# Windowed attention: the value product of a block moves from three blocks behind its scores to four

## The chip, the cores and the metric

The kernel runs on one core of a Trainium2 chip. The metric is the device time of one execution in microseconds. Before the change its median over three runs is 2266.35 us (2261.28 to 2271.24). TensorE (PE) multiplies matrices, VectorE (DVE), ScalarE (ACT) and GpSimd (POOL) work on rows, SyncE (SP) issues most transfers, and sixteen DMA engines carry them out.

## The reference, cut to what matters

One inference step of a two-layer network over 128 context tokens and 1024 latent tokens. The first layer mixes a state-space scan with pooling; the second has eight heads of differential attention over all keys and sixteen heads of windowed attention with a sink. The change concerns the last of these. For latent tokens a query block of 128 sees the context keys and its own and the two neighbouring key blocks:

```python
s_w = jnp.where(valid, s_w, NEG_INF)
s_c = jnp.einsum('bkgqd,bkld->bkgql', qb, k_ctx).astype(jnp.float32) * scale
logits = jnp.concatenate([s_c, s_w, jnp.broadcast_to(sk, s_c.shape[:-1] + (1,))], axis=-1)
p = jax.nn.softmax(logits, axis=-1).astype(v.dtype)
return (jnp.einsum('bkgql,bkld->bkgqd', p[..., :n_ctx], v_ctx)
        + jnp.einsum('bkgqw,bkwd->bkgqd', p[..., n_ctx:n_ctx + 3 * WIN_BLK], vw))
```

Context tokens attend to context tokens alone, with the same sink. Nothing of what is computed changes.

## The kernel before

The program is one long stream. The first layer takes about the first 950 us, its output projection and the start of the second layer follow; the eight dense (differential) heads run from about 1027 to 1697 us, the windowed heads, here called the sliding stage, from about 1698 to 2066 us, and the last output projection fills the rest.

**Numbers in two halves.** fp32 values are kept as a pair of fp16 tiles, high and low, and a product is three fp16 matmuls (`mm3`, lines 326 to 331, or the like). So a block of probabilities has a high and a low half.

**The sliding stage** is eight calls of `win_block` (line 1343), one for each pair of heads (`m` = 0, 1). A call walks nine query blocks, b0 (context) to b8. For each block TensorE makes the scores of both heads (lines 1367 and 1370), VectorE adds the mask and takes the extreme (1378; 1375 for b0), ScalarE takes exponentials into the fp32 tile `p` (1380), then copies `p` to fp16, the high half (1389), and GpSimd subtracts to get the low half (1390); both lie in `phl`. SyncE then issues a DMA transpose of `phl` into a tile `PT` (`transpose`, line 1233), of 4, 12 or 16 blocks of 128 x 128. Last, TensorE multiplies `PT` with the values (`win_pv`, lines 1407 to 1409) and ScalarE writes the result, scaled by the softmax's divisor, to `og` (1411). A finished pair is gated and written to DRAM (`go_dr`, line 1260).

**The lag.** The value product is not made at once. `win_block` puts it on the list `pend` (line 1392) and, in each block after the scores, calls `self.pop(2)`, which makes the oldest products until two are left. So in block b the product of block b - 3 is made. The list goes on over the change of pair.

**The filler.** Between these, TensorE is given slices of other projections (`F.take`), from a list of jobs: the next pair's Q first (`qk_block`, line 1158), then the gates (`z_block`). TensorE's order is as written; on the other engines a scheduler sets the order when the program is built, from its own estimate and from marks of priority. Each engine then runs its list strictly in order and waits by semaphores.

**The next pair's Q.** `qk_block` ends with four transfers on SyncE's queue (line 1198) that bring the finished Q, as `qhl`, into the layout that the scores need: two for `m` = 0 and then two for `m` = 1. They are called pieces 1 to 4. A score of head `m` reads all 128 partitions of `Q[:, m]`, so `m` = 0 needs pieces 1 and 2, `m` = 1 pieces 3 and 4.

**Buffers.** Tiles with one tag share a ring: before the change three of `p` (also used by the dense heads, line 1277, and by `cached_values`), three of `phl` and three of `PT`. A writer waits until the last reader of the ring's tile has finished.

Of the kernel before, what the change touches and what calls it, by code (L numbers as in the profile page):

```python
# [10 lines left out]
F32 = mybir.dt.float32  # L11
F16 = mybir.dt.float16
# [7 lines left out]
P = 128  # L20
TC = 128
TL = 1024
T = TC + TL
# [6 lines left out]
TK = T + TC  # L30
# [190 lines left out]
class Builder:  # L221
# [925 lines left out]
    def cached_values(self):  # L1147

        nc, A = self.nc, self.A
        self.cv = self.wt([P, 2, 10, P], F16, tag="cv", bufs=1)  # L1150
        cvf = self.cv.rearrange("p a b c -> p a (b c)")
        for c in (slice(0, TK // 2), slice(TK // 2, TK)):
            t = self.wt([P, T], F32, tag="p", bufs=3)[:, :TK // 2]
            nc.sync.dma_start(t, A["cv"][:, c])
            nc.scalar.activation(cvf[:, 0, c], t, AF.Copy)
            nc.vector.tensor_tensor(cvf[:, 1, c], t, cvf[:, 0, c], ALU.subtract)
# [71 lines left out]

    def transpose(self, phl, nb):

        pt = self.wt([P, 18, P], F16, tag="PT", bufs=3)
        with self.tc.high_priority():
            self.last_t = self.nc.sync.dma_start_transpose(pt[:, :nb], phl).ins
        if self.loads:
            with self.tc.issue_after(self.last_t):
                self.loads.popleft()()
        return pt
# [24 lines left out]
    def diff_head(self, h, F):  # L1262

        nc = self.nc
        F.until(("k", h))
        F.until(("q", h))
        k, q = self.R.pop(("k", h)), self.R.pop(("q", h))
        og = self.wt([P, NCH, P], F32, tag="og", bufs=3)
        oss = self.wt([P, 16], F32, tag="oss", bufs=2)
        left = F.left - (HEAD_KEEP if h < 7 else HEAD_LAST)  # L1270
        for b in range(NCH):
            nk = 1 if b == 0 else 9
            w = nk * P
            o = TC if b else 0
            qs = slice(b * P, (b + 1) * P)
            sm = self.wt([P, 16], F32, tag="sms", bufs=6)
            e = self.wt([P, T], F32, tag="p", bufs=3)[:, :w]


            for ms in ((0,), (1,)) if b else ((0, 1),):  # L1280
                st = self.pt("S", [P, 1536])
                out = self.pend.popleft()(st) if ms[0] == 0 and len(self.pend) > 2 else None
                sv = st[:, :len(ms) * w].rearrange("p (a b) -> p a b", b=w)
                for i, m in enumerate(ms):
                    for c0 in range(0, w, 512):
                        c1 = min(c0 + 512, w)
                        for x in range(2):
                            nc.tensor.matmul(sv[:, i, c0:c1], q[:, m, x, qs], k[:, m, o + c0:o + c1], start=x == 0, stop=x == 1)  # L1288
                with self.tc.high_priority():
                    nc.vector.tensor_reduce(out=sm[:, ms[0]:ms[-1] + 1], in_=sv, axis=AX.X, op=ALU.max, negate=True)  # L1290
                    for i, m in enumerate(ms):
                        nc.scalar.activation(sv[:, i] if m else e, sv[:, i], AF.Exp, bias=sm[:, m:m + 1],
                                             accum_out=sm[:, 4 + m:5 + m])
                if out is not None:
                    out()
                F.take(left / 16 if b else 2 * HEAD_FIRST)
            p = [e, sv[:, len(ms) - 1]]

            phl = self.wt([P, 2 * T], F16, tag="phl", bufs=3)
            with self.tc.high_priority():  # L1300
                nc.vector.reciprocal(sm[:, 6:8], sm[:, 4:6])
                nc.vector.scalar_tensor_tensor(sm[:, 2:3], sm[:, 4:5], self.nlam, sm[:, 7:8], ALU.mult, ALU.mult)
                nc.vector.scalar_tensor_tensor(p[0], p[1], sm[:, 2:3], p[0], ALU.mult, ALU.add)  # L1303
                nc.scalar.activation(phl[:, :w], p[0], AF.Copy)  # L1304
            nc.gpsimd.tensor_tensor(phl[:, w:2 * w], p[0], phl[:, :w], ALU.subtract)  # L1305
            pt = self.transpose(phl[:, :2 * w], 2 * nk)
            self.pend.append(lambda st=None, b=b, nk=nk, pt=pt, sm=sm: self.diff_pv(st, h, b, nk, pt, sm, og, oss))
# [35 lines left out]
    def win_block(self, qb, F):  # L1343

        nc = self.nc
        F.until(("wk", qb // 4))
        F.until(("q", 8 + qb))
        k, q = self.R["wk", qb // 4], self.R.pop(("q", 8 + qb))
        og = self.wt([P, NCH, P], F32, tag="og", bufs=3)
        kv = (qb // 2) % 2  # L1350
        fill = F.left / (2 * NCH - 2 + 2 * WIN_FIRST)
        for b in range(NCH):
            qs = slice(b * P, (b + 1) * P)
            if b == 0:
                lo, hi, nk, mk = 0, TC, 1, None
            else:
                lo, hi = max(b - 1, 1) * P, min(b + 2, NCH) * P
                nk = (hi - lo) // P + 1
                mk = self.mask[:, 1:4] if b == 1 else self.mask[:, 4:7] if b == 8 else self.mask[:, 0:4]
            w = nk * P  # L1360
            wl = hi - lo
            sm = self.wt([P, 16], F32, tag="sms", bufs=6)
            p = self.wt([P, T], F32, tag="p", bufs=3)[:, :2 * w]
            for m in range(2):
                s = self.pt("S1")
                for x in range(2):
                    nc.tensor.matmul(s[:, :wl], q[:, m, x, qs], k[:, kv, lo:hi], start=x == 0, stop=x == 1)  # L1367
                if b:
                    for x in range(2):
                        nc.tensor.matmul(s[:, wl:w], q[:, m, x, qs], k[:, kv, T:TK], start=x == 0, stop=x == 1)  # L1370
                nsk = self.nsink[:, 2 * qb + m:2 * qb + m + 1]
                nb = sm[:, m:m + 1]
                with self.tc.high_priority():
                    if mk is None:
                        nc.vector.tensor_reduce(out=nb, in_=s[:, :w], axis=AX.X, op=ALU.min)
                        nc.vector.tensor_tensor(nb, nb, nsk, ALU.min)
                    else:
                        nc.vector.tensor_tensor_reduce(out=s[:, :w], in0=s[:, :w], in1=mk.rearrange("p a b -> p (a b)"),  # L1378
                                                       scale=1.0, scalar=nsk, op0=ALU.add, op1=ALU.min, accum_out=nb)
                    nc.scalar.activation(p[:, m * w:(m + 1) * w], s[:, :w], AF.Exp, bias=nb, scale=-1.0,  # L1380
                                         accum_out=sm[:, 4 + m:5 + m])
                    nc.scalar.activation(sm[:, 6 + m:7 + m], self.row("sink", 2 * qb + m, 1), AF.Exp, bias=nb)  # L1382
            F.take(fill * WIN_FIRST if b == 0 else fill + WIN_SHIFT)
            self.pop(2)
            F.take(fill * WIN_FIRST if b == 0 else fill - WIN_SHIFT)
            nc.vector.tensor_reduce(out=sm[:, 2:4], in_=sm[:, 4:8].rearrange("p (a b) -> p b a", a=2), axis=AX.X, op=ALU.add)
            nc.vector.reciprocal(sm[:, 8:10], sm[:, 2:4])
            phl = self.wt([P, 2 * T], F16, tag="phl", bufs=3)
            nc.scalar.activation(phl[:, :2 * w], p, AF.Copy)  # L1389
            nc.gpsimd.tensor_tensor(phl[:, 2 * w:4 * w], p, phl[:, :2 * w], ALU.subtract)  # L1390
            pt = self.transpose(phl[:, :4 * w], 4 * nk)
            self.pend.append(lambda b=b, nk=nk, pt=pt, lo=lo, sm=sm: self.win_pv(qb, b, nk, lo, pt, sm, og))
# [262 lines left out]
```

## Time and profile before

| | us |
|---|---|
| median of three runs | 2266.35 (2261.28 to 2271.24) |
| profiled execution | 2267.45 |
| its span, first to last instruction | 2265.7 |
| mean granted TensorE clock | 0.957 |
| TensorE matmuls busy | 2022.8 (89%) |
| VectorE, ScalarE, GpSimd busy | 1467.3, 1224.6, 1062.4 |

A row of a group reads: line, engine, operation, what it writes and reads, count, busy time, mean of one in ns, idle time of the engine before it and what ended that. A row of time reads: start, duration, engine, line, operation; in brackets the idle time of the engine just before it and what released it. A row of a stretch reads: from:to, its length, busy time and count of PE, PEld, DVE, ACT and POOL, granted clock, share of the sixteen DMA engines, GB/s. A busy TensorE is not TensorE at its peak. SPq is SyncE's queue: the duration there is that of issuing, not of the transfer.

### The profile page before, as it was taken

To read this page: it belongs to the slowest core of one execution; us is meant where nothing else is said; L and a number is where in the kernel's file an instruction comes from. 1 tells how busy PE (TensorE), PEld (TensorE's weight loads), DVE (VectorE), ACT (ScalarE), POOL (GpSimd) and SP (SyncE) were. 2 spreads that over 40 slices of the span, in tenths; PEclk is the share of its full clock that TensorE was granted. 3 is DMA by queue.
4 is the path that set the end of the run, shared out by engine and by line. 5 is a ranking of instruction groups with operands and counts; after the bars stand their busy time and mean duration, and the time that the engine had idled before them with its cause. 6 is when DMAs were issued, how large, how long until landed. Compare 5 with 4: busy or idle time off the path is not lost. (4 is left out here: it accounts for less than half of the span.)

```text
span 2265.7 us, 49724 instructions
## 1 busy us (share of the span) xinstructions
PE 2022.8 (89%) x20258; PEld 1438.0 (63%) x20258; DVE 1467.3 (65%) x2722; ACT 1224.6 (54%) x2891; POOL 1062.4 (47%) x997
## 2 busy tenths in 40 slices
PE   5996788787989999998998998999889998998997
PEld 2654475564557655665676786776667777686566
DVE  5868989789586444675777767767755544552334
ACT  5565667566564322344665665565557867782321
POOL 1369677876675100144445445445346756651001
PEclk9998999998999999998999999999989999999999
DMA  7221523224657513034455555555457878899312
GB/s 277 73 81 48 138 72 99 77 89 127 198 205 209 184 66 109 26 124 109 103 121 115 113 120 114 111 116 120 103 117 133 170 148 157 167 175 216 139 47 84
DMA packets 435125, 283.10 MB, mean 125 GB/s; under 512 B 374448, under 2 KB 385232, under 8 KB 434896
## 3 DMA queue, kind: packets, MB, share of 16 engines
q1 hardware_dynamic: 433920, 279.34, 49.7%
q8 instruction: 158, 2.59, 0.5%
q10 hardware_dynamic: 976, 0.58, 0.1%
q14 instruction: 71, 0.58, 0.1%
HBM read 133.38 MB, written 29.05 MB: 72 GB/s over the span
## 5 line engine op out<-in xcount | busy, mean ns | idle before, releaser
L329 PE MATMUL psmm<-h,whl 128*128 128x384 f16 (+1 forms) x1104 | 367.8, 334 | 21.0 <-DVE q L1175 14.7
L330 PE MATMUL psmm<-h,whl 128*128 128x384 f16 (+1 forms) x1104 | 367.7, 334 | 2.3 <-DVE h L506 1.7
L331 PE MATMUL psmm<-h,whl 128*128 128x384 f16 (+1 forms) x1104 | 367.2, 333 | 0.0
L329 PE MATMUL psmm<-whl,h 128*128 128x128 f16 x1920 | 336.1, 221 | 10.4 <-DVE V L1211 10.4
L330 PE MATMUL psmm<-whl,h 128*128 128x128 f16 x1920 | 336.0, 221 | 0.0
L331 PE MATMUL psmm<-whl,h 128*128 128x128 f16 x1920 | 335.9, 221 | 0.0
L330 PEld LDWEIGHTS <-whl 128*128 128x128 f16 x2256 | 224.5, 100 | 165.2 <-issue 43.4
L331 PEld LDWEIGHTS <-whl 128*128 128x128 f16 x2256 | 224.4, 99 | 155.2 <-issue 15.8
L329 PEld LDWEIGHTS <-whl 128*128 128x128 f16 x2256 | 225.4, 100 | 145.7 <-issue 20.7
L1305 POOL TENSOR_TENSOR phl<-p,phl 128x1152 f16<-128x1152 f32 (+1 forms) x72 | 155.4, 2162 | 231.4 <-ACT phl L1304 231.4
L330 PEld LDWEIGHTS <-h 128*128 128x128 f16 x2520 | 247.5, 99 | 12.8 <-issue 11.1
L329 PEld LDWEIGHTS <-h 128*128 128x128 f16 x2520 | 247.5, 99 | 4.2 <-issue 2.6
L331 PEld LDWEIGHTS <-h 128*128 128x128 f16 x2520 | 247.5, 99 | 0.0
L323 DVE SCALAR_TENSOR_TENSOR whl<-w,whl 128x512 f16<-128x512 f32 x248 | 196.1, 809 | 64.5 <-ACT whl L322 63.5
L1290 DVE TENSOR_REDUCE sms<-psS 128x1 f32<-128x1152 f32 (+1 forms) x136 | 176.5, 1298 | 73.6 <-PE psS L1288 72.5
L1390 POOL TENSOR_TENSOR phl<-p,phl 128x1024 f16<-128x1024 f32 (+2 forms) x72 | 134.0, 1861 | 109.9 <-ACT phl L1389 77.4
L322 ACT ACTIVATE whl<-w 128x512 f16<-128x512 f32 x248 | 140.1, 609 | 79.2 <-PE psmm L331 42.6
L1288 PE MATMUL psS<-K,Q 128*128 128x512 f16 (+1 forms) x800 | 151.9, 326 | 32.1 <-DVE p L1303 17.1
L1180 POOL TENSOR_TENSOR sw<-sw,sin 128x384 f32<-128x384 f32 (+1 forms) x78 | 85.8, 1100 | 146.8 <-DVE sw L1179 128.0
L503 POOL TENSOR_TENSOR h<-mt,h 128x384 f16<-128x384 f32 (+2 forms) x32 | 29.1, 918 | 250.1 <-ACT h L502 250.1
L1288 PEld LDWEIGHTS <-Q 128*128 128x128 f16 x800 | 73.4, 99 | 100.5 <-DVE p L1303 18.1
L1304 ACT ACTIVATE phl<-p 128x1152 f16<-128x1152 f32 (+1 forms) x72 | 76.1, 1065 | 91.6 <-DVE p L1303 91.6
(382 smaller groups left out, 5877.2 us busy)
## 6 DMA issues: line engine op xcount, KB each, us to landing
w<-in_wod SPq DMA_DIRECT2D x52, 512.0 KB, 3.9
w<-in_wev SPq DMA_DIRECT2D x40, 512.0 KB, 4.0
E<-csrow SPq DMA_DIRECT2D x36, 512.0 KB, 4.5
Q<-qhl SPq DMA_DIRECT2D x64, 288.0 KB, 4.2
go_dr<-gl SPq DMA_DIRECT2D x15, 576.0 KB, 3.7
wada<-in_w_ada SPq DMA_DIRECT2D x32, 256.0 KB, 5.4
o<-in_w_ada SPq DMA_DIRECT2D x16, 512.0 KB, 5.6
xT<-in_w_ada SPq DMA_DIRECT2D x16, 512.0 KB, 5.7
```

The source lines that it names most:

```text
L322: nc.scalar.activation(hl[:, 0, a:e], w[:, a:e], AF.Copy if scale is None else AF.Identity, scale=sc)
L323: nc.vector.scalar_tensor_tensor(hl[:, 1, a:e], w[:, a:e], sc, hl[:, 0, a:e], ALU.mult, ALU.subtract)
L329: mm(out, ah, bh, start=start, stop=False)
L330: mm(out, ah, bl, start=False, stop=False)
L331: mm(out, al, bh, start=False, stop=stop)
L503: nc.gpsimd.tensor_tensor(h[:, 1, a:b], o, h[:, 0, a:b], ALU.subtract)
L1180: nc.gpsimd.tensor_tensor(sw[:, o:], sw[:, o:], self.sinT[:, a:b], ALU.mult)
L1288: nc.tensor.matmul(sv[:, i, c0:c1], q[:, m, x, qs], k[:, m, o + c0:o + c1], start=x == 0, stop=x == 1)
L1290: nc.vector.tensor_reduce(out=sm[:, ms[0]:ms[-1] + 1], in_=sv, axis=AX.X, op=ALU.max, negate=True)
L1304: nc.scalar.activation(phl[:, :w], p[0], AF.Copy)
L1305: nc.gpsimd.tensor_tensor(phl[:, w:2 * w], p[0], phl[:, :w], ALU.subtract)
L1390: nc.gpsimd.tensor_tensor(phl[:, 2 * w:4 * w], p, phl[:, :2 * w], ALU.subtract)
```

## The change

`win_block` calls `self.pop(3)` instead of `self.pop(2)`, so the product of block b - 4 is made in block b. Since one more transposed block is then alive, `PT` gets a fourth buffer, and to make room for it in SBUF the ring of fp32 probabilities `p` goes from three to two, for the dense heads, the cached values and the sliding heads.

```diff
@@ -1150,7 +1150,7 @@
-            t = self.wt([P, T], F32, tag="p", bufs=3)[:, :TK // 2]
+            t = self.wt([P, T], F32, tag="p", bufs=2)[:, :TK // 2]
@@ -1228,7 +1228,7 @@
-        pt = self.wt([P, 18, P], F16, tag="PT", bufs=3)
+        pt = self.wt([P, 18, P], F16, tag="PT", bufs=4)
@@ -1274,7 +1274,7 @@
-            e = self.wt([P, T], F32, tag="p", bufs=3)[:, :w]
+            e = self.wt([P, T], F32, tag="p", bufs=2)[:, :w]
@@ -1360,7 +1360,7 @@
-            p = self.wt([P, T], F32, tag="p", bufs=3)[:, :2 * w]
+            p = self.wt([P, T], F32, tag="p", bufs=2)[:, :2 * w]
@@ -1381,7 +1381,7 @@
             F.take(fill * WIN_FIRST if b == 0 else fill + WIN_SHIFT)
-            self.pop(2)
+            self.pop(3)
             F.take(fill * WIN_FIRST if b == 0 else fill - WIN_SHIFT)
```

Up to the sliding stage the instructions of all engines stand in the same order. In it they move, on TensorE as written and on SyncE by the scheduler.

TensorE, at the first change of pair: the value product of b8's turn and then the first scores of the next pair (`Q_21555`; `psS_2347` is head `m` = 0, `psS_2348` `m` = 1). Before, where `PT_21792` is the transpose of b5:

```order
L329 MATMUL psm_2325_21850<-whl_21563,h_10921 128x128
...
L1407 MATMUL pss_2341_22035<-V_20872,PT_21792 128x64
...
L1367 MATMUL psS_2347_22072<-K_20580,Q_21555 128x128
...
L1367 MATMUL psS_2348_22079<-K_20580,Q_21555 128x128
...
L329 MATMUL psmm_22094<-h_10914,whl_22089 128x384
```

And now, where `PT_21668` is the transpose of b4:

```order
L329 MATMUL psm_2324_21823<-whl_21563,h_10921 128x128
...
L1407 MATMUL pssm_22008<-V_20872,PT_21668 128x64
...
L1367 MATMUL psS_2346_22045<-K_20580,Q_21555 128x128
...
L1367 MATMUL psS_2347_22052<-K_20580,Q_21555 128x128
...
L329 MATMUL psmm_22067<-h_10914,whl_22062 128x384
```

The place of the product among the other matmuls is the same; it is of the block before, and the scores behind it are the same.

SyncE's queue at the same change of pair, from the transpose of b4 to that of b8. Before:

```order
L1233 DMA_TRANSPOSE PT_21689<-phl_21686 128x16x128
L1198 DMA Q_21555<-qhl_21552 64x2x1152 x2
L1233 DMA_TRANSPOSE PT_21792<-phl_21789 128x16x128
L1198 DMA Q_21555<-qhl_21552 64x2x1152 x2
L1233 DMA_TRANSPOSE PT_21895<-phl_21892 128x16x128
L1233 DMA_TRANSPOSE PT_21995<-phl_21992 128x16x128
L312 DMA w_2520_23664<-in_wod 128x1024
L1233 DMA_TRANSPOSE PT_22067<-phl_22064 128x12x128
```

And now:

```order
L1233 DMA_TRANSPOSE PT_21668<-phl_21665 128x16x128
L1198 DMA Q_21555<-qhl_21552 64x2x1152 x2
L1233 DMA_TRANSPOSE PT_21765<-phl_21762 128x16x128
L1198 DMA Q_21555<-qhl_21552 64x2x1152
L1233 DMA_TRANSPOSE PT_21868<-phl_21865 128x16x128
L1198 DMA Q_21555<-qhl_21552 64x2x1152
L1233 DMA_TRANSPOSE PT_21968<-phl_21965 128x16x128
L312 DMA w_2519_23637<-in_wod 128x1024
L1233 DMA_TRANSPOSE PT_22040<-phl_22037 128x12x128
```

Pieces 1 and 2 stand between the transposes of b4 and b5 in both. Pieces 3 and 4 stood together ahead of the transpose of b6; now piece 4 stands behind it. The same move is found at six of the seven changes of pair; at the fourth all four pieces stand together ahead of a transpose in both programs.

## The prediction

> **What bounds the kernel now.** I read the views from the whole down to one queue: the page's totals, stretches of the sliding stage, what TensorE waits for there, and then TensorE and the SyncE queue side by side over one change of pair (a pair is one call of `win_block`: two heads, nine query blocks, written b0 to b8).
>
> ```profile
> span 2265.7 us, 49724 instructions
> PE 2022.8 (89%) x20258; PEld 1438.0 (63%) x20258; DVE 1467.3 (65%) x2722; ACT 1224.6 (54%) x2891; POOL 1062.4 (47%) x997
> 1850.00:1950.00 100.00, 94.01 (x1273) 73.76 (x1271) 53.81 (x165) 72.77 (x204) 60.65 (x41) 0.97 0.75 147
> 1950.00:2050.00 100.00, 86.23 (x1399) 75.33 (x1396) 49.95 (x155) 75.92 (x216) 57.79 (x33) 0.94 0.98 184
> ```
>
> TensorE paces the kernel, and in the sliding stage (about 1700 to 2066 us) it still runs 86 to 94% of the time, while the last columns of such a row (granted clock, share of the sixteen DMA engines, GB/s) show the transfers filling up: 0.75, then 0.98. The instruction stream before this stage stands in the same order in both programs, so the stage is where the time can change. What TensorE waits for (total, times, longest), first from 1700 to 2020 us with all seven changes of pair, then, after the dots, in the last pair:
>
> ```profile
> PE psS L1367 <- DMA Q<-qhl: 11.2, 6, 2.4
> PE pss L1407 <- DMA PT<-phl: 7.3, 4, 2.4
> PE pssm L1407 <- DMA PT<-phl: 3.0, 1, 3.0
> PE psS L1367 <- ACT sms L1382: 2.8, 1, 2.8
> ...
> PE pss L1407 <- DMA PT<-phl: 4.9, 2, 4.5
> PE pssm L1407 <- DMA PT<-phl: 2.3, 3, 1.6
> ```
>
> There are two kinds. A value product (L1407) waits for its transposed probabilities: 10.3 us at five changes of pair and 7.2 in the last pair, 17.5 in all, and this is what the change touches. The first scores of a pair (L1367) wait for that pair's Q: 11.2 us, and 2.8 put down to ScalarE at the same place of the second change, 14.0 at all seven. How the two stand to each other is seen at the first change of pair, TensorE first and then SyncE's queue:
>
> ```profile
> 1733.84 0.20 PE L1407 MATMUL pss<-V,PT 128*128 128x64 f16 x1 [1.05 <-DMA PT<-phl]
> 1734.55 0.28 PE L1367 MATMUL psS<-K,Q 128*128 128x128 f16 x2
> 1737.15 0.27 PE L1367 MATMUL psS<-K,Q 128*128 128x128 f16 x2 [2.33 <-DMA Q<-qhl]
> ...
> 1723.02 3.12 SPq L1233 DMA_TRANSPOSE PT<-phl  x1
> 1726.19 1.28 SPq L1198 DMA_DIRECT2D Q<-qhl  x2
> 1727.78 3.57 SPq L1233 DMA_TRANSPOSE PT<-phl  x1
> 1731.40 1.75 SPq L1198 DMA_DIRECT2D Q<-qhl  x2
> 1733.26 7.74 SPq L1233 DMA_TRANSPOSE PT<-phl  x2
> ```
>
> The value product of b5 waits 1.05 us for the transpose issued at 1727.78; 0.7 us later the scores of head m = 0 go through (Q pieces 1 and 2, issued at 1726.19), and those of m = 1 wait 2.33 us for pieces 3 and 4, issued from 1731.40. The wait for Q comes last here and sets when TensorE goes on.
>
> **The change, part by part.**
>
> *Value products one block later.* Nothing is added or removed on TensorE. In b8 it now runs the product of b4, whose transpose (1723.02) landed long before, so the 1.05 us goes, and TensorE reaches the m = 1 scores that much sooner. But they cannot start before Q piece 4 is there: what the first wait loses, the second gains. Worth 0 at a change of pair, whatever the size of the first wait; bounds: -1.05 if Q came sooner, 0 else. I take 0.
>
> *Q piece 4 goes behind a transpose.* In six of the seven changes of pair (not the one from the fourth to the fifth, where all four pieces go before the transpose) SyncE's queue now reads: pieces 1 and 2, transpose of b5, piece 3, transpose of b6, piece 4, transpose of b7. Before, piece 4 went ahead of the transpose of b6. So one transpose more stands before the piece that ends the wait. Its price:
>
> ```profile
> 1730.89:1734.30 3.41, 2.36 (x50) 2.14 (x47) 1.51 (x8) 3.41 (x12) 1.03 (x1) 1.00 1.07 204
> 1734.30:1737.72 3.42, 1.09 (x22) 0.78 (x18) 1.01 (x4) 2.15 (x7) 1.09 (x1) 1.00 1.03 199
> 1737.72:1741.13 3.41, 3.41 (x17) 1.53 (x15) 2.97 (x10) 2.62 (x10) 0.17 (x1) 0.50 1.01 140
> 2056.79 6.95 SPq L1233 DMA_TRANSPOSE PT<-phl  x3
> 2061.83 0.20 PE L1407 MATMUL pss<-V,PT 128*128 128x64 f16 x1 [0.37 <-DMA PT<-phl]
> 2064.34 0.20 PE L1407 MATMUL pssm<-V,PT 128*128 128x64 f16 x1 [1.64 <-DMA PT<-phl]
> DMA to landing us min/median/max: 3.2/4.2/5.1
> ```
>
> The engines are full around the wait (share 1.07, 1.03, 1.01), so one transfer more ahead is its whole duration more. A transpose of 16 blocks is 128 x 16 x 128 x 2 bytes = 524 KB; at the 199 to 204 GB/s of these rows 2.6 us. The last pair gives the same from another side: three transposes issued back to back, and TensorE is released by two of them at 2061.83 and 2064.34, 2.51 us apart. To that I add 0.2 us, an estimate for the new hand-over: piece 4 is issued only when the transpose's issue has ended, and it needs its own 3.2 us (shortest row of Q's landings) from there. Bounds: 2.4 us (the transfer alone, starting slightly sooner since piece 4 no longer runs before it) and 4.5 us (half of the 7.74 us that the two issues from 1733.26 took is 3.9, plus the 0.6 of piece 4's own issue). I take 2.8, near the lower end, since the transfer has two rows and the issue time only overlaps it. Six times 2.8 is **16.8 us**. No cover: TensorE stands in its queue in front of exactly these scores, earlier than before. The transpose of b6 does not hold piece 4 longer by being unready, since its input is done at 1730.8, about 1.5 us before its new place in the queue (after piece 3, half of the 1.75 us from 1731.40):
>
> ```profile
> 1728.66 2.13 POOL L1390 TENSOR_TENSOR phl<-p,phl 128x1024 f16<-128x1024 f32 x1 [0.91 <-ACT phl L1389]
> ```
>
> Behind the wait on TensorE stand the next pair's projections and value products; ScalarE's exponentials of the next b0 wait with it, and behind them the fp16 copy of b8 and its transpose. All of these have a block or more in hand and move along; the next pair's own Q begins with TensorE's scores of that pair, so the delay is not won back but passed on.
>
> *The clock.* In 1737.72 to 1741.13 the granted clock is 0.50: after the wait TensorE runs one such stretch at half speed, which costs 1.7 us. The new wait is about 1.05 + 2.33 + 2.8 = 6.2 us in one piece, nearly two stretches. It may put the slow stretch partly inside the wait (down to -1.7) or keep it a second time (up to +1.7); I take 0.
>
> *Two buffers of fp32 probabilities instead of three.* An exponential now needs the GpSimd subtraction of two blocks earlier, not three. The tightest places in the dense and in the sliding stage, subtraction first:
>
> ```profile
> 1190.38 2.75 POOL L1305 TENSOR_TENSOR phl<-p,phl 128x1152 f16<-128x1152 f32 x2 [7.72 <-ACT phl L1304]
> 1193.40 1.22 ACT L1292 ACTIVATE p<-psS,sms 128x1152 f32<-128x1152 f32 x1 [0.41 <-DVE sms L1290]
> 2015.20 1.64 POOL L1390 TENSOR_TENSOR phl<-p,phl 128x768 f16<-128x768 f32 x1 [6.39 <-ACT phl L1389]
> 2018.43 0.58 ACT L1380 ACTIVATE p<-psS,sms 128x384 f32<-128x384 f32 x1 [1.60 <-DVE sms L1378]
> ```
>
> The first row merges two subtractions; even the end of both (1193.13) comes before the exponential at 1193.40, and the one that matters is the first of them. In the sliding stage 2016.84 stands against 2018.43, 1.6 us. So both are hidden, 0. If the cover were gone, ScalarE would wait some tenths of a us at one block of each dense head, under 3 us in all.
>
> *The fourth buffer of transposes* lets a transpose be issued while four products are open; the product that frees it still runs in the same block, so SyncE gains nothing and loses nothing.
>
> *The end of the stage.* In the last pair transposes and loads of gated outputs alternate:
>
> ```profile
> 2050.03 0.23 PE L1407 MATMUL pss<-V,PT 128*128 128x64 f16 x1 [4.51 <-DMA PT<-phl]
> ```
>
> This wait (4.51) goes, but the product of b7 at 2064.34 hangs on the seventh transpose of a full queue, and before that one stand the same transfers in both programs. TensorE arrives sooner and waits there: 0, bounds -4.5 and +1.
>
> **Sum.** 0 + 16.8 + 0 + 0 + 0 + 0 = +16.8 us on the profiled execution's 2267.45 us (span 2265.7 and 1.75 around it): 2284.3. The median of the runs shown is 1.1 below that execution, so **2283 us**. With 2.4 to 3.4 us a change and the clock 1 us either way on each, 2274 to 2293 is this forecast's own range.
>
> **Rivals.**
>
> *A. The waits on transposes simply vanish and Q is in time.* Then 17.5 us go: 2249. For it: such waits at five of seven changes of pair. Against it: every change of pair has a wait for Q, which at the one shown comes 0.7 us later, and Q's place in the queue gets worse. The Trainium skill, Perfetto Trace Analysis (Identifying Performance Opportunities), says that a gap repeating on the engine that should be saturated can mean that there is no room for the next tile, buffer count included; by that rule the fourth buffer is the cure and the time falls. The trace agrees as to the repeating gap; what a buffer does to it no run here shows yet.
>
> *B. Traded waits, about no change.* Piece 4 is half the size of the transpose ahead of it, and if the sixteen engines let it pass, its lateness is 0 to 1 us and the sum 0 to 6: 2266 to 2272, say 2268. Against it: the share above 1.0, which leaves no engine idle to let it pass. The Trainium skill, DMA: Bandwidth & Descriptors (Queues, rings and completion order), says that an engine takes descriptors in ring order but that a later one may finish its write before an earlier one; by it this case is possible, and no run here shows it.
>
> *C. Much slower.* The whole issue time of the transpose delays piece 4 (4.5 us) and each longer wait keeps the clock low for a second stretch (1.7): 6 x 6.2 = 37, 2303. For it: long waits elsewhere (the 4.51 above). Against it: the issue time overlaps the transfers ahead.
>
> **How the numbers follow.** Forecast 0.66, A 0.10, B 0.19, C 0.05. 0.5% (about 11.3 us, what a measurement of this kernel can tell from no change) above 2266.35 is 2277.7. Of the forecast some 0.60 lies above that and 0.06 under it, C adds 0.05, B lies within, A is faster for 0.08 and within for 0.02: slower 0.65, same 0.27, faster 0.08. The range 2264 to 2294 leaves out A, C and the edges of B and of the forecast, under 2 in 10.
>
> **What would show it.** Right: in the changed profile the waits of L1407 at changes of pair are gone, the waits of L1367 for Q have grown from 14.0 us to about 14 + 10 + 17 = 41 (10 is what the products' waits just before them held), unchanged at the fourth change of pair, and the stage is some 17 us longer while everything before 1700 us stands as it was. Step by step: piece 4's landing minus piece 3's is near 4 us (a transpose and a piece); no ScalarE exponential waits for GpSimd's L1305 or L1390; half-clock stretches are as many as before. Wrong: waits for Q that stay near 2 us (B), a stage that is shorter (A), or a transpose of b6 that SyncE holds back for a buffer.

## The result and the profile after

| | before | after |
|---|---|---|
| median | 2266.26 us (2261.28 to 2271.24, 6 runs) | 2288.85 us (2285.56 to 2289.81, 6 runs) |
| ratio, 95% interval | | 1.0096 (1.0082 to 1.0111) |
| profiled execution, its span | 2267.45, 2265.7 us | 2289.31, 2287.5 us |
| mean granted clock | 0.957 | 0.954 |

The change makes the kernel 22.6 us slower. 2283 was forecast, as a loss of 16.8 us; 2288.85 lies inside the forecast's own range.

The page's totals after:

```profile
span 2287.5 us, 49750 instructions
PE 2023.7 (88%) x20258; PEld 1435.4 (63%) x20258; DVE 1478.8 (65%) x2722; ACT 1225.1 (54%) x2891; POOL 1061.1 (46%) x997
```

The same two stretches of the sliding stage as in the prediction:

```profile
1850.00:1950.00 100.00, 90.69 (x1303) 73.85 (x1301) 50.06 (x151) 70.28 (x197) 59.24 (x39) 0.97 0.75 156
1950.00:2050.00 100.00, 84.28 (x1280) 72.08 (x1278) 50.17 (x151) 71.18 (x203) 55.28 (x34) 0.91 0.80 153
```

TensorE is busy for as long as before (2022.8 then, 2023.7 now): the 22 us are waiting, and nearly all of them lie in the sliding stage. It starts 1.2 us earlier than before (1697.04 against 1698.23), and its last change of pair ends 20.0 us later (2031.26 against 2011.23); what follows is 1.8 us longer. What TensorE waits for, from 1700 to 2040 us (all seven changes of pair), and after the dots in the last pair:

```profile
PE psS L1367 <- DMA Q<-qhl: 40.4, 7, 7.4
PE psS L1367 <- ACT p L1380: 5.1, 10, 0.6
PE psS L1367 <- ACT zs L1222: 0.8, 1, 0.8
...
PE pssm L1407 <- DMA PT<-phl: 4.0, 1, 4.0
PE pss L1407 <- DMA PT<-phl: 3.4, 1, 3.4
```

The value products (L1407) wait at no change of pair any more; in the last pair they wait 7.4 us, where it was 7.2. The waits for Q have grown from 14.0 to 40.4 us (41 was forecast). One kind is new: scores that wait for a PSUM bank to be emptied by an exponential, twice in each of five pairs, 5.1 us.

The first change of pair, the scores on TensorE and then SyncE's queue:

```profile
1731.65 0.28 PE L1367 MATMUL psS<-K,Q 128*128 128x128 f16 x2
1738.33 0.37 PE L1367 MATMUL psS<-K,Q 128*128 128x128 f16 x2 [6.40 <-DMA Q<-qhl]
...
1724.10 1.28 SPq L1198 DMA_DIRECT2D Q<-qhl  x2
1726.19 3.76 SPq L1233 DMA_TRANSPOSE PT<-phl  x1
1729.99 0.60 SPq L1198 DMA_DIRECT2D Q<-qhl  x1
1730.70 3.72 SPq L1233 DMA_TRANSPOSE PT<-phl  x1
1734.47 0.60 SPq L1198 DMA_DIRECT2D Q<-qhl  x1
```

TensorE comes to the `m` = 1 scores 2.9 us earlier than before (0.28 us behind 1731.65, where it was 0.28 us behind 1734.55) and goes on 1.2 us later. Piece 3 is issued at 1729.99, piece 4 only at 1734.47, with a whole transpose between: TensorE stands still for 6.40 us where the prediction said 6.2.

### The profile page after: what moved, and what is told of

The parts are those of the page before. It is cut to its first block, busy times and chain, and to the rows that moved or that the text cites. A ratio compares the mean times of both kernels' runs of the same rounds, so it can differ in the third digit from the quotient of the medians.

```text
span 2287.5 us, 49750 instructions
## 1 busy us (share of the span) xinstructions
PE 2023.7 (88%) x20258; PEld 1435.4 (63%) x20258; DVE 1478.8 (65%) x2722; ACT 1225.1 (54%) x2891; POOL 1061.1 (46%) x997
## 5 line engine op out<-in xcount | busy, mean ns | idle before, releaser
L323 DVE SCALAR_TENSOR_TENSOR whl<-w,whl 128x512 f16<-128x512 f32 x248 | 204.9, 845 | 68.8 <-ACT whl L322 55.8
L1288 PEld LDWEIGHTS <-Q 128*128 128x128 f16 x800 | 73.1, 98 | 98.3 <-DVE p L1303 16.8
L1380 ACT ACTIVATE p<-psS,sms 128x512 f32<-128x512 f32 (+2 forms) x144 | 90.4, 628 | 80.2 <-DVE sms L1378 45.1
```

Source lines behind the costliest of these rows:

```text
L323: nc.vector.scalar_tensor_tensor(hl[:, 1, a:e], w[:, a:e], sc, hl[:, 0, a:e], ALU.mult, ALU.subtract)
```

## The experiments

The theory to test: a piece of Q that stands behind one more transpose on SyncE's queue comes 2.8 us later, at six of seven changes of pair, and that is the loss; the lag and the buffers as such cost nothing. A rival came from the trace after. In five pairs the scheduler had also moved an instruction on VectorE: the first half of a weight split (`load_w`, L323) now runs ahead of the mask operations (L1378) of b4, and the prediction had put no price on it. The split in the second pair before, and GpSimd's subtraction at that time:

```profile
1758.75 0.69 DVE L323 SCALAR_TENSOR_TENSOR whl<-w,whl 128x512 f16<-128x512 f32 x1
1756.60 2.13 POOL L1390 TENSOR_TENSOR phl<-p,phl 128x1024 f16<-128x1024 f32 x1 [0.48 <-ACT phl L1389]
```

The same after, with the mask operation that now follows:

```profile
1759.55 1.83 DVE L323 SCALAR_TENSOR_TENSOR whl<-w,whl 128x512 f16<-128x512 f32 x1
1761.30 0.75 DVE L1378 CUSTOM_DVE_ANT_0 psS<-psS,mask,nsink 128x512 f32<-128x512 f32 x1
1758.69 2.13 POOL L1390 TENSOR_TENSOR phl<-p,phl 128x1024 f16<-128x1024 f32 x1 [0.64 <-ACT phl L1389]
```

Before, the split started when the subtraction had ended (1758.73) and took 0.69 us; now it starts in the middle of it, ends 0.55 us behind it and takes 1.83, and the mask operations of b4 come behind.

The kernels that differ in the lag, the buffers and the place of Q's pieces (the other five medians stand with their experiments), each ratio with the runs of before on the same chip:

| kernel | median | ratio (95% interval) | waits for Q | of products | for a bank |
|---|---|---|---|---|---|
| before | 2266.26 | 1 | 14.0 | 10.3 | 0 |
| after | 2288.85 | 1.0096 (1.0082 to 1.0111) | 40.4 | 0 | 5.1 |
| lag 4, piece 4 ahead of b6's transpose | 2269.06 | 1.0011 (0.9998 to 1.0025) | 25.1 | 0 | 5.1 |
| lag 3, piece 4 behind b6's transpose | 2285.21 | 1.0077 (1.0064 to 1.0090) | 31.0 | 8.9 | 0 |
| lag 3, the change's buffers | 2265.24 | 0.9992 (0.9982 to 1.0003) | 17.2 | 7.3 | 0 |
| lag 4, all of Q ahead of b5's transpose | 2249.45 | 0.9927 (0.9914 to 0.9941) | 3.8 | 3.1 | 8.9 |
| lag 3, all of Q ahead of b5's transpose | 2273.90 | 1.0031 (1.0019 to 1.0043) | 2.6 | 24.7 | 0 |

(Waits of TensorE from 1700 us to the end of the last change of pair, in us; those put down to ScalarE's `sms` at a Q place are counted as waits for Q, as in the prediction.)

A trace shows one execution. Those of experiments 1 and 10 took 5.9 and 7.2 us more than their medians (2274.92 and 2266.23 us), so their waits are those of a longer execution. And in the twelve profiles the stage starts between 1692.25 and 1698.94 us, although the same instructions stand ahead of it in the same order. A few us between two traces therefore show nothing unless they are found inside the stage.

### 1. Piece 4 first again

```diff
-                    nc.sync.dma_start(d[...], hl[...])
+                    self.qd = nc.sync.dma_start(d[...], hl[...]).ins
...
-            pt = self.transpose(phl[:, :4 * w], 4 * nk)
+            with self.tc.issue_after(self.qd) if b == 6 and qb < 7 else ExitStack():
+                pt = self.transpose(phl[:, :4 * w], 4 * nk)
```

> The changed kernel with one thing undone: the transpose of b6 is queued on SyncE behind Q piece 4 again, in all seven changes of pair, as before the change; all other engines keep the order of the changed kernel. Theory (piece 4 behind the transpose costs some 2.5 us at each of six changes, the rest of the 22.6 us comes from VectorE's weight split that now runs ahead of the mask operations of b4): 15 us less than the changed kernel, about 2274, waits for Q at the m = 1 scores down from 40.4 to about 25 us, the ten short waits of scores for a free bank (5.1 us) unchanged. Rival 1 (SyncE's order is all of the loss): 2266, as before. Rival 2 (SyncE's order is worth nothing, VectorE or the p ring makes the loss): 2289, as the changed kernel.

Measured: 2269.06 us. What TensorE waits for at the changes of pair:

```profile
PE psS L1367 <- DMA Q<-qhl: 25.1, 7, 4.6
PE psS L1367 <- ACT p L1380: 5.1, 10, 0.6
```

SyncE's order alone takes back 19.8 of the 22.6 us. Rival 2 falls. The waits came out as expected, 25.1 us: the 14.0 of before, the 10.3 that the products had held, and 0.8. The time came out nearer to rival 1. So the lag of four has taken every wait of the products away, and the time has not gone down for it. And the bank waits stand here in full, with the time at most 5.7 us (the interval's end) above before: VectorE's move is worth less than the 7 us that the theory had left for it. (At the fourth change the edit also moved the transpose of b6 behind the four pieces, which neither kernel has; the wait there is 3.02 us, 2.39 before.)

### 2. Piece 4 late, nothing else

```diff
+                    def dq(m=m, x=x): return nc.sync.dma_start(d[...], hl[...])
+                    if m and x and key[1] > 8 and key[1] != 12:
+                        self.q4 = dq
+                    else:
+                        dq()
...
             pt = self.transpose(phl[:, :4 * w], 4 * nk)
+            if b == 6 and qb < 7 and qb != 3:
+                with self.tc.issue_after(self.last_t):
+                    self.q4()
```

Piece 4 is kept back as `q4` and issued behind the transpose of b6.

> The kernel before with one thing done: Q piece 4 is issued behind the transpose of b6 in the same six changes of pair; value products stay three blocks behind, buffers stay, VectorE keeps its order. Theory: the wait for Q grows by about 2.5 us at six changes and nothing covers it, 2266 + 15 = 2281. Rival 1 (SyncE's order is all of the loss): 2289. Rival 2 (it is worth nothing): 2266.

Measured: 2285.21 us, 17.5 above the 2267.66 of before on this chip. The waits (lines stand four to seven higher in this kernel):

```profile
PE psS L1371 <- DMA Q<-qhl: 31.0, 7, 5.9
PE pss L1414 <- DMA PT<-phl: 5.1, 3, 2.5
PE pssm L1414 <- DMA PT<-phl: 3.8, 2, 2.1
```

The loss is made without the change, by the place of one transfer. The waits for Q grow by 17.0 us, which is 2.8 on the mean of six changes (1.4 to 4.7 at single ones), the price that the prediction had put on it; the products' waits shrink by 1.4.

### 3. The buffers alone

```diff
-            self.pop(3)
+            self.pop(2)
```

> The changed kernel with the value products three blocks behind again: only the buffers of the change are left (two of fp32 probabilities, four of transposed ones). Theory: 2266 within 2 us, no new wait of an exponential for GpSimd's subtraction outside the last pair. Rival (two buffers of p hold ScalarE back in dense heads and in the last pair): up to 5 us more, 2271.

Measured: 2265.24 us, no difference that can be told (0.9982 to 1.0003). No exponential waits for GpSimd's subtraction in the dense heads or in the sliding stage. The ring of two is hidden, as forecast. VectorE keeps the order of before here, so its move comes with the lag. One place of SyncE's queue did change: at the fourth change of pair piece 4 stands behind the transpose of b7, and the wait there is 5.24 us where it was 2.39.

### 4. VectorE's split behind the mask operations

```diff
+                with self.tc.issue_after(self.x4) if late and a == 0 else ExitStack():
                     nc.vector.scalar_tensor_tensor(hl[:, 1, a:e], w[:, a:e], ...)
```

Here `x4` is the mask operation of b4, and `late` is set for the weights of four of the five pairs.

> The changed kernel with the first half of VectorE's weight split (L323 there) queued behind the mask operations of b4 again in four of the five pairs where it had moved ahead (the second, third, fifth and sixth); the scheduler then also issues the shuffle of Q's last chunk ahead of those mask operations in these pairs, so that Q's last pieces are ready earlier than in either kernel. SyncE still issues piece 4 behind the transpose of b6. Theory: the ten short bank waits (5.1 us) fall to about 1 us and the Q chain starts 2 us earlier in these pairs: 6 to 9 us less than the changed kernel, about 2281. Rival 1 (SyncE's order is all of the loss): 2289, unchanged. Rival 2 (VectorE's order is all of it): 2268 or less.

Measured: 2289.84 us (1.0084 to 1.0110), as after. The waits:

```profile
PE psS L1370 <- DMA Q<-qhl: 47.1, 7, 8.4
PE psS L1370 <- ACT p L1384: 1.0, 2, 0.6
```

The bank waits go, as expected, and the time stays: the waits for Q take up 6.7 us more. That looks like "VectorE is worth nothing", but it is not a clean test. In these four pairs the scheduler also moved Q's first piece ahead of the transpose of b4, so that a transpose stands between each two pieces, and on GpSimd Q's subtraction ahead of that of b4's probabilities.

### 5. All of Q ahead of the transpose of b5

The edit, against the kernel of experiment 1:

```diff
-            with self.tc.issue_after(self.qd) if b == 6 and qb < 7 else ExitStack():
+            with self.tc.issue_after(self.qd) if b == 5 and qb < 7 else ExitStack():
```

> The changed kernel (products four blocks behind) with all four Q pieces queued on SyncE ahead of the transpose of b5, in every change of pair; other engines as in the changed kernel. Theory (the wait for Q ends when piece 4 lands, and that is set by how many transposes of 2.5 to 3 us stand before it; the products have a block of slack): one transpose less than in the run with piece 4 ahead of the transpose of b6, so its 25.1 us of waits for Q fall by 2.9 us at six changes to about 8, and the time from 2269 to about 2252. Rival 1 (the transposes of b5 to b7, each a piece or two later, now make products wait): waits of L1407 of 10 us or more come back, 2262 to 2268. Rival 2 (Q is not ready sooner, order within the queue is no longer the limit): 2269.

Measured: 2249.45 us, 0.7% faster than before (0.9914 to 0.9941) and 39.4 us faster than the changed kernel, from which it differs by the order of SyncE's queue alone. What TensorE waits for at the changes of pair (the products' line is one higher here):

```profile
PE psS L1367 <- ACT p L1380: 8.9, 15, 0.8
PE psS L1367 <- DMA Q<-qhl: 3.8, 2, 2.1
PE pssm L1408 <- DMA PT<-phl: 1.6, 2, 1.0
PE pss L1408 <- DMA PT<-phl: 1.5, 2, 1.1
```

SyncE's queue at the first change of pair, with the four pieces in one row between the transposes of b4 and b5:

```profile
1717.09 2.27 SPq L1233 DMA_TRANSPOSE PT<-phl  x1
1719.43 3.67 SPq L1198 DMA_DIRECT2D Q<-qhl  x4
1723.21 10.46 SPq L1233 DMA_TRANSPOSE PT<-phl  x3
```

A stretch of 100 us with two changes of pair in it:

```profile
1750.00:1850.00 100.00, 95.37 (x1346) 76.81 (x1345) 54.73 (x169) 76.14 (x216) 66.66 (x43) 1.00 0.89 170
```

The queue is a scale: with the last piece of Q behind two transposes (b5 and b6), one, or none, the same kernel takes 2288.85, 2269.06 and 2249.45 us, 19.8 and 19.6 apart. The waits for Q do not follow as evenly (40.4, 25.1, 3.8), and part of the last step is the clock (1.00 in the row, against 0.95 in experiment 1, 0.93 after and 0.97 before in the stretch from 1750 to 1850): more on it below.

The scale holds for six changes of pair. At the fourth all four pieces stand behind the transposes of b5 and b6 before, after and here, where the edit moved nothing; the longest wait for Q that is left, 2.12 us, stands there.

### 6. The same with the products three blocks behind

The edit of 5 on the kernel before.

> The kernel before (products three blocks behind) with all four Q pieces queued ahead of the transpose of b5, in every change of pair. Theory: here the product of b5 runs in b8, just ahead of the scores that need Q, so the transpose that is delayed by two pieces (2.6 us) makes the product wait longer by what Q gains: waits for Q fall from 14.0 to under 3 us, waits of products rise from 10.3 to about 23, time 2266 within 4 us. Rival (the product has slack): 2252, and then the fourth block is of no use.

Measured: 2273.90 us, 7 us slower than before (4.3 to 9.7) and so some 4 us beyond what was expected; the waits came as expected.

```profile
PE pss L1408 <- DMA PT<-phl: 16.3, 4, 4.6
PE pssm L1408 <- DMA PT<-phl: 8.4, 2, 4.4
PE psS L1367 <- DMA Q<-qhl: 2.6, 1, 2.6
```

With a lag of three, the product of b5 runs right ahead of the new pair's scores, so a transpose that comes later makes the product wait for what Q has gained: waits for Q from 14.0 to 2.6, waits of products from 10.3 to 24.7. Here is what the fourth block is good for: under this order of the queue it is worth 24.5 us (2273.90 to 2249.45), under the order before it was worth nothing (2267.66 to 2269.06).

### 7. Both: Q ahead and the split behind

The edits of 4 and 5 together.

> The kernel with all four Q pieces ahead of the transpose of b5 and products four blocks behind, and beside it the first half of the weight split on VectorE queued behind the mask operations of b4 in four of five pairs; there the shuffle of Q's last chunk goes ahead of them too, and piece 1 goes even before the transpose of b4. Theory: the ten waits for a free bank fall from 5.1 to 1 us, and Q, ready 2 us sooner, ends its wait altogether: 3 to 8 us less than with all Q pieces ahead alone, about 2247. Rival (VectorE's order matters nowhere, since what it saves is waited for elsewhere): the same time as that kernel, 2252.

Measured: 2257.41 us (0.9941 to 0.9968), 8 us slower than with Q ahead alone. Neither expectation held. Bank waits fall to 1.9 us, but the waits at Q's places are back (8.5 us put down to Q and 5.2 to ScalarE).

### 8. Pieces 3 and 4 from ScalarE's queue

```diff
-                    nc.sync.dma_start(d[...], hl[...])
+                    (nc.scalar if m and key[1] > 8 else nc.sync).dma_start(d[...], hl[...])
```

> The changed kernel with Q pieces 3 and 4 issued from ScalarE's queue instead of SyncE's (pieces 1 and 2 and all transposes stay on SyncE); ScalarE spends some 1.2 us a pair on the two issues. Theory A (the loss is the order in one queue: a piece on another queue does not wait for the transposes ahead): pieces 3 and 4 land 3 us or more sooner than in the changed kernel, waits for Q fall from 40.4 to below 25, 2255 to 2270. Theory B (the loss is full engines whatever the queue): the pieces share the engines with the transposes and land little sooner, waits for Q stay above 35, 2283 to 2289.

Measured: 2262.73 us (0.9969 to 0.9989). No wait for Q is left; in their place stand 17.2 us of waits for a bank and others for ScalarE:

```profile
PE psS L1367 <- ACT p L1380: 17.2, 23, 1.5
PE pssm L1407 <- ACT og L1411: 3.4, 3, 1.2
```

Where the pieces were issued, on ScalarE's queue and on SyncE's, at the first change of pair:

```profile
1722.67 2.18 ACTq L1198 DMA_DIRECT2D Q<-qhl  x2
...
1722.67 1.29 SPq L1198 DMA_DIRECT2D Q<-qhl  x2
1730.68 4.85 SPq L1233 DMA_TRANSPOSE PT<-phl  x2
```

The time is that of theory A, but the run does not decide between A and B: with ScalarE's order changed, the transpose of b5 was itself issued only at 1730.68, so all four pieces had free way, and nothing shows how a piece fares on another queue beside a transpose.

### 9 and 10. The split behind, with SyncE's queue held

To part VectorE's order from SyncE's, the edit of 4 was made with the queue pinned: once to the order of the changed kernel (9), once to that of experiment 5 (10). The queue's part of the edit in 9:

```diff
+            with self.tc.issue_after(self.qd) if b in (5, 6, 7) and qb < 7 and qb != 3 else ExitStack():
                 pt = self.transpose(phl[:, :4 * w], 4 * nk)
+            for _ in range({4: 2, 5: 1, 6: 1}.get(b, 0) if self.q4 else 0):
+                with self.tc.issue_after(self.last_t):
+                    m, x, piece = self.q4.pop(0)
+                    piece(m, x)
```

> The changed kernel with the first half of VectorE's weight split behind the mask operations of b4 in four of the five pairs where it had moved ahead (the shuffle of Q's last chunk then goes ahead of them too), and with SyncE's queue held at the order of the changed kernel: pieces 1 and 2 behind the transpose of b4, piece 3 behind that of b5, piece 4 behind that of b6. In the earlier run with this VectorE order piece 1 had moved up a place and each piece stood behind one transpose more, so that what Q gained was given back. Theory (VectorE's order is the rest of the loss, 1.4 us by the run with SyncE's order restored, 3.6 by the run with piece 4 late alone): 2285 to 2287, bank waits from 5.1 to 1 us, waits for Q about 41. Rival (the two us by which Q is ready earlier shorten each wait at four changes): 2280. Rival 2 (nothing, as TensorE waits for piece 4 anyway): 2289 within 1.5.

> The fastest kernel so far (products four blocks behind, all four Q pieces ahead of the transpose of b5, 2249.5) with the same VectorE order as the run before it, SyncE's queue unchanged. In that kernel hardly any wait for Q is left that could swallow what VectorE saves: of its 16 waits of scores for a free bank (9.6 us) some 0.4 to 1.3 us a pair lie right behind the split in four pairs. Theory: 2 to 5 us less, 2245 to 2247. Rival (VectorE's order is worth nothing): 2249 within 1.5. Rival 2 (as in the earlier run with this VectorE order, where piece 1 also went ahead of the transpose of b4: waits for Q come back): 2257.

Measured: 2293.49 us (1.0090 to 1.0134) and 2259.08 us (0.9949 to 0.9978), so 4.6 and 9.6 us slower than the kernels that they vary. The first difference is not clear of noise, as its interval overlaps that of the changed kernel (1.0082 to 1.0111); the second is. In 9 every expectation missed. In 10 the time is that of rival 2, and waits for Q did come back (17.8 us), but not for its reason, since piece 1 was held in its place. Undone in this way, VectorE's move saves nothing. In experiment 9 TensorE waits for:

```profile
PE psS L1376 <- DMA Q<-qhl: 50.5, 9, 9.2
PE psS L1376 <- ACT p L1390: 1.0, 2, 0.6
```

GpSimd in its second pair, with Q's subtraction first:

```profile
1761.11 2.38 POOL L1193 TENSOR_TENSOR qhl<-q,qhl 128x1152 f16<-128x1152 f32 x1 [1.27 <-ACT qhl L1192]
1763.44 4.23 POOL L1400 TENSOR_TENSOR phl<-p,phl 128x1024 f16<-128x1024 f32 x2
```

And in the changed kernel, with that of b4's probabilities first:

```profile
1765.75 2.13 POOL L1390 TENSOR_TENSOR phl<-p,phl 128x1024 f16<-128x1024 f32 x1
1767.84 2.38 POOL L1188 TENSOR_TENSOR qhl<-q,qhl 128x1152 f16<-128x1152 f32 x1
```

The bank waits go again (5.1 to 1.0), and the waits for Q rise from 40.4 to 50.5. With the shuffle of Q's last chunk earlier, GpSimd takes Q's subtraction ahead of that of b4's probabilities, whose transpose stands at the head of this part of SyncE's queue. That the later transpose is what delays Q fits, but was not tried by itself. VectorE's move could not be undone alone, so its price stays open.

## Why the prediction was right, point by point

**The value product's move is worth nothing at a change of pair** ("what the first wait loses, the second gains"): shown. The waits of L1407 are gone, and with piece 4 back in its place (experiment 1) the waits for Q are the old ones plus those 10.3 us, and the time is that of before within its interval. Rival A (2249, Q in time) falls for the change as it is. Its number came out where Q was put in time, in experiment 5, but by chance: A had only the products' 17.5 us in it, while about half of experiment 5's gain is clock (last section).

**Piece 4 behind a transpose, 2.8 us at six changes, 16.8 in all**: shown by experiment 2, 17.5 us of time and 17.0 of waits. Rival B (a transfer that overtakes the transpose) falls with it, and C falls as a sum (6.2 us a change). The price was right, but it is made up otherwise than the working had it, where the issue time only overlapped the transfer. On the mean of the six changes piece 4 is issued 4.5 us behind piece 3, where it was 0.8, and TensorE goes on 3.8 us after that issue, where it was 4.8. So 3.7 us of later issue, of which C was right to speak, are partly won back by 1.0 us of quicker landing. Piece 4 lands some 4.6 us behind piece 3 at the first change (piece 3 lands 3.7 us after 1729.99, and TensorE goes on at 1738.33), where near 4 was said. The fourth change, where the four pieces stay together, waits 1.57 us (2.39 before), a little less, where no change was said.

**The clock, 0**: right as a sum. From the start of the stage to the end of the last change of pair the clock is halved for 26.3 us before and 40.7 after, but the longer waits lie in these stretches. TensorE was busy for 23.1 and 24.3 us of them, so they cost half of that, 11.6 and 12.1 us. "As many as before" was wrong for the stretches, right for the loss.

**Two buffers of `p`, 0**: right by experiment 3. The step "no ScalarE exponential waits for GpSimd" was wrong in two places of the changed kernel:

```profile
1746.94 0.58 ACT L1380 ACTIVATE p<-psS,sms 128x384 f32<-128x384 f32 x1 [0.67 <-POOL phl L1390]
2039.88 0.58 ACT L1380 ACTIVATE p<-psS,sms 128x384 f32<-128x384 f32 x1 [2.59 <-POOL phl L1390]
```

Both are the b1 right behind a wait for Q, when blocks that had piled up come in quick succession; neither is there in experiments 1, 2, 3 and 5.

**The end of the stage, 0**: right, 7.2 us of waits before and 7.4 after.

**What was missing.** The forecast was 5.8 us short of the median (2283 to 2288.85). The sum "0 + 16.8 + 0 + 0 + 0 + 0" has no term for the order on VectorE and ScalarE, and the trace shows ten bank waits of 5.1 us behind the split. For them speaks the account of the two profiled executions: up to the end of the last change of pair the stage is 21.2 us longer after (313.0 to 334.2), and the waits have changed by 26.4 (Q), -10.3 (products) and 5.1 (bank), which is 21.2 as well. But whether they are the missing term is not shown: what the change costs beside the late piece is 3.6 us by the medians of experiment 2 (2285.21 to 2288.85) and 1.4 us by those of experiment 1 (2267.66 to 2269.06), with some 3 us either way on each.

## What to carry to other kernels

A wait that ends at the same place as a later one is worth nothing by itself: before paying for a deeper lag, find the wait that ends last there, and what stands ahead of it in its queue. A deeper lag is worth something when it lets other work be put off. Here it freed a transpose to be issued later, and only with Q ahead of that transpose did it bring 24.5 us, while the same order without it lost 7. After a change of lag or buffers, read the order of every in-order queue again, since the scheduler may have put the transfer that is waited for behind one that has time.

## What the runs showed of the hardware

**The clock falls by fixed stretches, not by long pauses.** In experiment 5 two waits of 0.7 and 2.1 us, 0.3 us apart at the fourth change of pair, brought the one half-clock stretch between 1700 and 2030 us. The two rows (TensorE's busy time stands behind the length, the granted clock ahead of the last two numbers):

```profile
1865.25:1868.66 3.41, 0.87 (x23) 0.60 (x19) 2.23 (x5) 2.38 (x6) 1.64 (x1) 1.00 1.17 155
1868.66:1872.07 3.41, 3.16 (x12) 1.68 (x13) 2.53 (x7) 1.99 (x8) 0.60 (x1) 0.50 1.20 153
```

In experiment 10 a stretch with more work in it, 1.41 us, was still followed by half the clock:

```profile
1878.51:1881.92 3.41, 1.41 (x11) 0.91 (x12) 2.79 (x6) 1.70 (x7) 1.21 (x1) 1.00 1.13 213
1881.92:1885.34 3.42, 3.42 (x33) 2.26 (x32) 1.70 (x5) 2.45 (x8) 1.35 (x2) 0.50 0.96 129
```

In experiment 7 one with 1.60 us was not:

```profile
1955.10:1958.51 3.41, 1.60 (x12) 1.04 (x13) 2.04 (x7) 2.19 (x8) 0.92 (x1) 1.00 1.10 191
1958.51:1961.93 3.42, 3.42 (x44) 2.43 (x43) 1.94 (x6) 3.42 (x12) 1.18 (x1) 1.00 1.14 215
```

Every change of the clock lies on one grid of 3.41 us. On it, in the twelve profiles of this case, 63 full-clock stretches that begin between 1700 and 2030 us had TensorE busy for up to 1.47 us (that one from 1931.23 in the changed kernel), and each was followed by one at half clock; none with 1.60 us or more was. Some records of TensorE may be missing, so the bound is read as "between 40 and 50% of a stretch". The Trainium skill, TensorE: Matmul & The Clock Gate (Why this matters for your kernels), asks for no idle gaps over about 3 us; here shorter ones were enough, where 2.5 us of them fell into one stretch. This is a good part of experiment 5's gain. From the start of the stage to the end of the last change of pair, 313.0 us before and 296.0 there, the loss to the clock was 11.6 us and is 2.7, 8.9 of the 17.0 us; TensorE's idle time in pauses over 0.3 us fell from 25.0 to 16.4 us. Some 5 us are given back after it.

**VectorE stands still beside GpSimd.** Each weight split of the sliding stage that began while GpSimd ran a subtraction (but for those that began in its last 0.03 us), in three profiles (before, after, experiment 5), ended 0.55 us behind it, whatever was left: it took 1.13 to 2.48 us instead of 0.69. The mask operation, which reads one of its two tensors from PSUM, was not held: all 96 of this size took 0.74 to 0.76 us in each of the three profiles, though more than half began beside a busy GpSimd. One of them (before, beside the subtraction that ends at 1758.73):

```profile
1757.41 0.75 DVE L1378 CUSTOM_DVE_ANT_0 psS<-psS,mask,nsink 128x512 f32<-128x512 f32 x1
```

The Trainium skill, GPSIMD Engine Reference (Specifications), says that the two engines share SBUF interfaces and that they contend when a VectorE instruction has two SBUF inputs, as the split has. The trace agrees, and shows the form that it takes here: not a slower run but a halt until the other is done.
